# A decoder step on one core: the second column block's weights are loaded ahead of the query, key and value weights

## The chip, the core and the metric

The kernel runs on one core of a Trainium2 chip. A core has a tensor engine (PE, which multiplies and transposes; PEld is its loading of weights), a vector engine (DVE), a scalar engine (ACT), a general engine (POOL, which also starts the indirect gathers) and an engine that starts the ordinary DMA transfers (SP). Each works through its own list of instructions in order, and waits on the others by semaphores. The metric is the device time of one execution in microseconds (us).

## The reference

One layer of a decoder, for a prompt of 1024 tokens and for a sample of 8 sequences with 8 new tokens each, which also read 8192 cached positions in pages:

```
n = rmsnorm(h, g_mix)
u = n @ w_in                                     # one projection: columns of GLA q, k, v, gate, rank; MLA latents
gq, gk, gv, gg, ga, mq, mkv, mkr = split(u)
o_gla = rmsnorm(gla_chunked(gq, gk, gv, decay(ga))) * silu(gg)
qf = rmsnorm(mq) @ mla_w_qup                     # 8 heads: 64 plain + 32 rotary columns, each normalised
ckv, krope = rmsnorm(mkv), rope(rmsnorm(mkr))
k, v = from ckv @ mla_w_kvup, krope              # also for every cached page of the sample
o_mla = attention(q, k, v)
h = h + [o_gla, o_mla] @ w_o
h = h + conv_ffn(rmsnorm(h))                     # gated, causal convolution of width 3
h = h + (p @ ple_w_proj) * sigmoid(rmsnorm(h) @ ple_w_gate)
```

## The kernel before

**Arithmetic.** Products are made in fp32r, with each operand split into a high and a low part. `split` casts the high part on ACT (L138) and subtracts it from the source on DVE, or on POOL where the caller says so (L139). `mm3` then makes three matmuls: high by high (L162), low by high (L163), high by low (L164).

**Two streams.** The program is written as two generators. The cache stream goes over 64 blocks of the paged cache (8 sequences of 8 blocks). Per block it gathers 128x1024 values (`craw`) and 128x256 (`krraw`) through POOL's queue (L496), transposes them (L545), multiplies them by the key weights (`ks`, L162 to L164), and does scores (`csr`), exponentials and sums; `chl` (L626 on ACT, L628 on POOL) is the split of a block's latents for its last product, 128x1024 elements. The dense stream makes the first and the second half of the prompt (`prompt_half(0)`, `prompt_half(1)`), then GLA and prompt attention. A loop takes a step of the one or the other: each dense step yields a number (7.2, 2.0, ...) that says how much of the tensor engine it is worth, and the cache stream's due time advances by 4.4 times a pace per step. This sets the order in which the program is written. A scheduler then gives each engine its list: of the instructions that are ready by its own estimate, the one written first goes first. So a load that is written earlier has precedence over those that are now written behind it, on SP and, with its cast and its subtraction, on ACT and POOL.

**The half prompt.** `prompt_half` normalises and transposes the tokens into `xTh`, `xTl` (8 x 128 rows by 512 tokens), makes the latents `lat` (`ps_lt`), and goes on by column blocks of `w_in` of 128 columns. `load_mix` fetches a block's weights with two DMAs of 128x4x128 (256 KB each, L180, into `stage`), casts them on ACT and subtracts on POOL; the product `ps_pj` is eight steps of `mm3`, 128x512 each. In the first half, each block is also multiplied by the sample's rows (`ps_sm`, L309); `gsf` (L313, L315) gathers the result, and `pt_gvs` (L854) transposes it. The order is given by `PLAN`:

```
PLAN = ([0], [], [1, 2, 3])
```

Block 0 comes first, then `rank()` (`pt_ga`, L869), the norms of the latents, the loads of the query weights (`load_q`: four pieces of 128x384, L180, low parts on DVE) and of the key and value weights (`load_kv`: two pieces of 128x512, DVE), and then, for each tile of 128 tokens, the transposes of its latents (`latents_T`: `pt_cq`, L925), one column block (1, 2, 3, and none with the last tile) and the tile's heads (`ps_q`, `ps_kv`). The weight tiles `w` share a pool of three buffers, the `stage` tiles one of three.

**The sample's opening.** In the first half, the sample's query is made between block 0 and block 1. `q_finish` normalises it on DVE: `rsqrt` (L123, L124, L125 on `nwt`, `qrs`), then the plain part `qt` by its reciprocal norm (L350) and gain (L351), and the rotary part (L353, L354). `sample_absorb` transposes it on the tensor engine (`pt_q`, L439), copies it on ACT to `qT_s` (L440), multiplies it by the absorbed key weights (`ps_qp`, L443), and transposes the rotary part (`pt_qr`, L449). The casts of L454 on POOL (`mv1h`, `mv1l`) copy the split key weights for the odd sequences.

Of the kernel before, what the change touches and what calls it, by code (L numbers as in the profile page):

```python
# [18 lines left out]
P = 128  # L19
# [48 lines left out]
def step_kernel(ctx: ExitStack, tc: tile.TileContext, A):  # L68
# [97 lines left out]
    def wload(wp, src, kc, n, tag, bufs=None, sbufs=2, st=None, lo_eng=None, out=None):  # L166

        if out is None:
            hi = wp.tile([P, kc, n], F32R, tag=tag + "h", name=tag + "h", bufs=bufs)
            lo = wp.tile([P, kc, n], F32R, tag=tag + "l", name=tag + "l", bufs=bufs)  # L170
        else:
            hi, lo = out
        sv = src.rearrange("(k p) c -> p k c", p=P)
        nc_ = n if n <= 512 else (512 if n % 512 == 0 else 384)
        ks = max(d for d in range(1, kc + 1) if kc % d == 0 and d * nc_ <= 512)
        for k0 in range(0, kc, ks):
            for c0 in range(0, n, nc_):
                raw = st([P, ks, nc_], F32) if st else wp.tile([P, ks, nc_], F32, tag="stage", name="stage", bufs=sbufs)
                cs = slice(c0, c0 + nc_)
                sp.dma_start(raw, sv[:, k0:k0 + ks, cs])  # L180
                split(hi[:, k0:k0 + ks, cs], lo[:, k0:k0 + ks, cs], raw, lo_eng)
        return hi, lo
# [77 lines left out]
    def wtile():  # L260
        return wp.tile([P, 2 * D], F32R, tag="w", name="w")

    def wpair(kc, n):

        w = wtile()
        return tuple(w[:, s * kc * n:(s + 1) * kc * n].rearrange("p (k c) -> p k c", c=n) for s in range(2))

    def load_q():
        return [wload(wp, A["mla_w_qup"][0][:, f * 384:(f + 1) * 384], 2, 384, "w", sbufs=3, out=wpair(2, 384))
                for f in range(2)]  # L270

    def load_kv():
        hl = [wk.tile([P, 1, D], F32R, tag="xin", name="wkv") for _ in range(2)]
        return [w[:, 0] for w in wload(wp, A["mla_w_kvup"][0], 1, D, "w", sbufs=3, out=hl)]

    def load_mix(c0, lo_eng=pool):

        w = wtile().rearrange("p (k s c) -> p k s c", k=8, s=2)
        hl = wload(wp, w_in[:, c0:c0 + P], 8, P, "w", sbufs=3, lo_eng=lo_eng, out=(w[:, :, 0], w[:, :, 1]))
        return hl + (w,)  # L280
# [255 lines left out]
    turned_c, ahead, loads = [], [0], [0]  # L536
# [204 lines left out]
    def prompt_half(hf):  # L741
# [5 lines left out]
        def proj(w, n, st=None):  # L747
            ps = pd([P, 512], "ps_pj")
            for k in range(8):
                mm3(ps[:n], w[0][:, k, :], w[1][:, k, :], xTh[:, k, :], xTl[:, k, :], k == 0, k == 7)  # L750
            if st is None:
                st = wk.tile([P, 512], F32, tag="st", name="st", bufs=3)
            act.copy(st[:n], ps[:n])
            return st
# [78 lines left out]

        def gates(G, G0):

            with tc.high_priority():
                for x in [G, ggs] + G0:
                    tc.keep_in_program_order(act.activation(x, x, AF.Silu))
                tc.keep_in_program_order(act.preload_act_table_set("natural_log_exp_and_others"))
            put_gates(G, hs)  # L840
            for x, t in zip(G0, (0, 256)):
                put_gates(x, slice(t, t + 256))

        def put_gates(G, ts):
            sp.dma_start(dgg[:, ts].rearrange("(c p) t -> p c t", p=P), G)

        def post(c, st, w, G=None):
            c0 = c * P
            if c < 4:
                sp.dma_start(dgqk[c0:c0 + P, hs], st)  # L850
            if hf == 0:
                t = proj_sample(w, pd)
                pt = pd([P, 512], "pt_gvs")
                pe.transpose(pt[:, :R], t, ident[:R, :R])  # L854
                act.copy(gqT[:, c, :] if c < 4 else ggs[:, c - 8, :], pt[:, :R])
                if c == 11:
                    put_gates(G, hs)
            elif c == 8:
                for t in (0, 256):
                    x = wk.tile([P, 4, 256], F32, tag="xin", name="G0")  # L860
                    sp.dma_start(x, dgg[:, t:t + 256].rearrange("(c p) t -> p c t", p=P))
                    G0.append(x)

        G0 = []

        def rank():
            pt = pd([P, 4, P], "pt_ga")
# [7 lines left out]
        def norm_latents(i):  # L875
            t = 4 * hf + i
            tt = slice(t * P, (t + 1) * P)
            l = lat[:, i, 16:NL]
            latents(l, P, ropep[:, t, :], l[:, 0:256], l[:, 256:384], l[:, 384:416])
            sp.dma_start(A["ckv_p"][tt, :], l[:, 256:384])  # L880
            sp.dma_start(A["krope_p"][tt, :], l[:, 384:416])

        def mix(chunks, G=None):
            prev = None
            for c in chunks + [None] * bool(chunks):
                if c is not None:
                    w = load_mix(c * P)
                    st = proj(w, P, G[:, c - 8] if c >= 8 else None)
                    if c == 11 and hf > 0:
                        gates(G, G0)  # L890
                if prev is not None:
                    post(*prev, G)
                prev = (c, st, w)
                yield (5.3 if hf else 7.2) if c is not None else 0.3
# [36 lines left out]
        def heads(i, cTh, cTl):  # L931
# [31 lines left out]
            yield 1.3  # L963

        yield from mix(PLAN[0])
        rank()
        for i in range(4):
            norm_latents(i)
        yield from mix(PLAN[1])
        wq = load_q()  # L970
        wkh, wkl = load_kv()
        for i in range(4):
            cT = latents_T(i)
            yield from mix(PLAN[2][i:i + 1])
            yield from heads(i, *cT)
# [403 lines left out]
    def dense():  # L1379
        for hf in range(2):  # L1380
            z["part"] = 2 * hf
            if hf:
                z["gla"] = gla_weights()
            yield from prompt_half(hf)
        den.close()
        wa2 = const.tile([17, 256], F32, tag="gtile", name="wa2")
        sp.dma_start(wa2[0:1], A["gla_b_a"])
        sp.dma_start(wa2[1:17], A["gla_w_a2"][0])
        with ExitStack() as s2:
            g, g2 = (s2.enter_context(tc.tile_pool(name=nm, bufs=2, reuse_waits="tile")) for nm in ("g", "g2"))  # L1390
            z["part"] = 4
            sample = gla_sample(g, wa2, *z["gla"])
            for n, w in enumerate(gla_prompt(g2, wa2, *z["gla"])):
                yield w
                if n > GS0:
                    z["part"] = 5
                    w2 = next(sample, None)
                    if w2 is not None:
                        yield w2
            for w in sample:  # L1400
                yield w
        with ExitStack() as s2:
            ap = s2.enter_context(tc.tile_pool(name="ap", bufs=2, reuse_waits="tile"))
            z["part"] = 6
            yield from prompt_attention(ap)
        z["part"] = 7
        wo_room()
# [229 lines left out]
    while live_c or live_d:  # L1637
# [4 lines left out]
        else:  # L1642
            w = next(dn, done)
# [307 lines left out]
    with tc.issue_after(z["phl"].ins):  # L1951
# [4 lines left out]
        for i, r in enumerate(raws45):  # L1956
            f, c = i // 2, 4 + i % 2
# [888 lines left out]
```

## Time and profile before

| | before |
|---|---|
| runs, us | 2199.25, 2199.87, 2206.59 (median 2199.87) |
| the profiled execution, us | 2198.96 |
| its span, us | 2197.3 |
| mean granted clock of the tensor engine | 0.987 |
| PEld busy | 1901.9 us, 87% |
| DMA | 244.55 MB, 111 GB/s over the span |

The span goes from the first to the last instruction of the profiled execution; its own time is 1.7 us more. A busy time is the sum over an engine's instructions; the share is of the span. In a list of instructions in order of time, a row gives start, duration (us), engine, line, operation, result<-operands, size, type, count, and in brackets how long the engine had stood idle before and which instruction released it. In a list of waits, the three numbers behind a row are the idle time, how often, and the longest. In a table by stretches, a row gives the stretch (us), its length, then busy time and number of instructions of PE, PEld, DVE, ACT and POOL, then PE's granted clock, the share of DMA and GB/s.

### The profile page before, as it was taken

What the parts mean: (1) busy time and instruction counts of PE and PEld (TensorE: products, weight loads), DVE (VectorE), ACT (ScalarE), POOL (GpSimd) and SP (SyncE); (2) the same over time, 40 slices, a digit from 0 to 9 for tenths busy, and PEclk for the clock granted to TensorE, in tenths of its full rate; (3) what the DMA queues carried; (4) which work ended last, traced back from release to release, by engine and by line L of the source; (5) the groups of instructions that cost most, each with busy time, mean ns of one, the idle gap of its engine ahead of it and who ended that gap; (6) DMA issues with size and microseconds to landing.
All of it is one profiled execution on the core that took longest, in us unless ns stands there. A gap on an engine that the chain in (4) does not pass through costs nothing. (4 is left out here: it accounts for less than half of the span.)

```text
span 2197.3 us, 37407 instructions
## 1 busy us (share of the span) xinstructions
PE 2121.5 (97%) x12928; PEld 1901.9 (87%) x12928; DVE 1704.0 (78%) x2611; ACT 1384.2 (63%) x3735; POOL 1229.4 (56%) x1348
## 2 busy tenths in 40 slices
PE   7999999999999999999999999999999999999998
PEld 6888978878888888887898978999999999888787
DVE  4775667377778888887788888788888886887795
ACT  5676766777778888887777776443333334434761
POOL 6675668576677777767454656556566562011211
PEclk9999999999999999999999999999999999999999
DMA  5343245422342222221431223232322325778642
GB/s 184 109 142 111 72 124 159 131 70 61 104 125 65 61 68 66 62 62 42 164 91 61 68 74 118 90 110 82 98 91 93 100 92 193 221 219 245 195 145 84
DMA packets 203576, 244.55 MB, mean 111 GB/s; under 512 B 42940, under 2 KB 137260, under 8 KB 203388
## 3 DMA queue, kind: packets, MB, share of 16 engines
q1 hardware_dynamic: 184428, 181.39, 26.3%
q0 software_dynamic: 17728, 56.31, 8.7%
q10 hardware_dynamic: 1232, 4.46, 0.6%
q8 instruction: 104, 1.70, 0.3%
q14 instruction: 84, 0.69, 0.1%
HBM read 196.39 MB, written 45.67 MB: 110 GB/s over the span
## 5 line engine op out<-in xcount | busy, mean ns | idle before, releaser
L583 ACT ACTIVATE csq<-ks 128x256 f32<-128x256 f32 x1040 | 392.8, 401 | 93.7 <-PE ks L164 82.0
L588 DVE TENSOR_REDUCE css<-csq 128x16 f32<-128x1024 f32 (+1 forms) x264 | 315.7, 1196 | 60.4 <-ACT csq L583 59.2
L138 ACT CAST wh<-st 128x512 fp32r<-128x512 f32 x164 | 100.9, 619 | 169.9 <-PE ps_gu L163 157.6
L162 PE MATMUL ks<-mv0h,cTh 128*128 128x320 f32 (+1 forms) x520 | 171.5, 332 | 7.4 <-ACT sn L585 3.7
L162 PE MATMUL ks<-mv1h,cTh 128*128 128x320 f32 (+1 forms) x520 | 170.1, 329 | 7.6 <-ACT sn L585 3.6
L628 POOL TENSOR_TENSOR chl<-craw,chl 128x1024 fp32r<-128x1024 f32 x64 | 141.5, 2211 | 55.4 <-ACT chl L626 54.8
L163 PE MATMUL ks<-mv1l,cTh 128*128 128x320 f32 (+1 forms) x520 | 153.8, 298 | 0.0
L163 PE MATMUL ks<-mv0l,cTh 128*128 128x320 f32 (+1 forms) x520 | 152.7, 295 | 0.0
L164 PE MATMUL ks<-mv0h,cTl 128*128 128x320 f32 (+1 forms) x520 | 148.2, 298 | 0.9 <-DVE cTl L139 0.8
L164 PE MATMUL ks<-mv1h,cTl 128*128 128x320 f32 (+1 forms) x520 | 148.4, 299 | 0.1
L656 POOL TENSOR_TENSOR phl<-sn,phl 128x512 fp32r<-128x512 f32 (+1 forms) x63 | 84.0, 1334 | 83.1 <-ACT phl L653 82.6
L139 DVE TENSOR_TENSOR wl<-st,wh 128x512 fp32r<-128x512 f32 x124 | 108.6, 879 | 25.8 <-ACT wh L138 25.7
L139 POOL TENSOR_TENSOR wl<-st,wh 128x512 fp32r<-128x512 f32 x40 | 62.0, 1550 | 104.9 <-ACT wh L138 100.1
L163 PE MATMUL ps_dn<-o 128*128 128x512 f32 x308 | 120.2, 390 | 0.1
L164 PE MATMUL ps_dn<-o 128*128 128x512 f32 x308 | 120.2, 390 | 0.0
L139 DVE TENSOR_TENSOR cTl<-ctp,cTh 128x512 fp32r<-128x512 f32 (+1 forms) x136 | 90.0, 662 | 37.5 <-ACT cTh L138 36.5
L162 PEld LDWEIGHTS ks<-mv0h,cTh 128*128 128x128 f32 x520 | 98.6, 190 | 21.4 <-ACT sn L585 8.1
L585 ACT COPY sn<-ks 128x64 f32<-128x64 f32 x520 | 116.8, 225 | 0.0
L162 PEld LDWEIGHTS ks<-mv1h,cTh 128*128 128x128 f32 x520 | 99.3, 191 | 19.8 <-ACT sn L585 7.4
L1333 POOL TENSOR_TENSOR pl<-p,ph 128x512 fp32r<-128x512 f32 (+1 forms) x96 | 97.5, 1020 | 32.7 <-DVE ph L1332 22.7
L162 PE MATMUL ps_dn<-o 128*128 128x512 f32 x308 | 115.8, 391 | 0.0
L164 PE MATMUL ps_gu<-xrh,wl 128*128 128x320 f32 x352 | 108.8, 309 | 0.0
(744 smaller groups left out, 7760.9 us busy)
## 6 DMA issues: line engine op xcount, KB each, us to landing
raw<-ds SPq DMA_DIRECT2D x77, 256.0 KB
raw<-ffn_w_down SPq DMA_DIRECT2D x66, 256.0 KB
stage<-w_in SPq DMA_DIRECT2D x48, 256.0 KB
wr<-ffn_w_down SPq DMA_DIRECT2D x44, 256.0 KB
st<-ffn_w_gate SPq DMA_DIRECT2D x42, 256.0 KB
st<-ffn_w_up SPq DMA_DIRECT2D x42, 256.0 KB
ds<-cv SPq DMA_DIRECT2D x19, 512.0 KB
oraw<-doT SPq DMA_DIRECT2D x16, 256.0 KB
```

Source lines behind the costliest of these rows:

```text
L138: cast = act.copy(hi, src)
L139: res = (lo_eng or dve).tensor_tensor(lo, src, hi.bitcast(F32), ALU.subtract)
L162: pe.matmul(ps, ah, bh, start=first, stop=False)
L163: pe.matmul(ps, ah, bl, start=False, stop=False)
L164: return pe.matmul(ps, al, bh, start=False, stop=last)
L583: act.activation(sq[:, f * 256:f * 256 + 256], ks[:, 0:256], AF.Square)
L585: act.copy(o.sn[:, g0 + i, :], ks[:, 256:320])
L588: dve.tensor_reduce(o.ss[:, g0 + i + 1 - n:g0 + i + 1, :].rearrange("p i h -> p (i h)"), sq2[:, :n].rearrange("p i (h n) -> p (i h) n", n= ...
L628: pool.tensor_tensor(ch[:, c0:c1, 128:256], src, ch[:, c0:c1, 0:128].bitcast(F32), ALU.subtract)
L656: (dve if drain == 2 else pool).tensor_tensor(phl[:, :nt, 64:128], sb, phl[:, :nt, 0:64].bitcast(F32), ALU.subtract)
L1333: pool.tensor_tensor(pl[:, c0:], p[:, c0:], ph[:, c0:].bitcast(F32), ALU.subtract)
```

## The change

In the first half of the prompt, the weights of column block 1 are loaded ahead of the query, key and value weights, and kept until the block's turn comes; its product stays where it was written, behind the transposes of the first tile's latents. The second half is as before.

```diff
--- before.py
+++ after.py
@@ -861,7 +861,7 @@
                     sp.dma_start(x, dgg[:, t:t + 256].rearrange("(c p) t -> p c t", p=P))
                     G0.append(x)
 
-        G0 = []
+        G0, ahead = [], {}
 
         def rank():
             pt = pd([P, 4, P], "pt_ga")
@@ -884,7 +884,7 @@
             prev = None
             for c in chunks + [None] * bool(chunks):
                 if c is not None:
-                    w = load_mix(c * P)
+                    w = ahead.pop(c) if c in ahead else load_mix(c * P)
                     st = proj(w, P, G[:, c - 8] if c >= 8 else None)
                     if c == 11 and hf > 0:
                         gates(G, G0)
@@ -967,6 +967,8 @@
         for i in range(4):
             norm_latents(i)
         yield from mix(PLAN[1])
+        if hf == 0:
+            ahead[1] = load_mix(P)
         wq = load_q()
         wkh, wkl = load_kv()
         for i in range(4):
```

Every engine gets the same instructions as before, in another order: on the tensor engine from the first `pt_cq` on, up to about its 6300th of 12692 instructions, and the same from there on. Lines behind L970 are two higher in the changed kernel.

On SP the loads of the block come ahead of those of the query weights (the numbers behind `stage` count the tiles as the program writes them):

```order
-L180 DMA stage_893<-mla_w_qup 128x384
+L180 DMA stage_893<-w_in 128x4x128
 L382 DMA krope_s<-krs_117 64x32
 L503 DMA newk_111<-krs_117 8x32
 L422 DMA wkr_554<-mla_w_kvup 128x1024
-L180 DMA stage_897<-mla_w_qup 128x384
+L180 DMA stage_897<-w_in 128x4x128
 L180 DMA stage_902<-mla_w_qup 128x384
 L180 DMA stage_906<-mla_w_qup 128x384
```

The first two query pieces made room, and are now issued behind these rows.

On POOL, in the opening, the subtractions of the block (`w_892`) come between the gather of a cache block and the casts of L454, ahead of L628:

```order
 L496 DMA craw_719<-cache_ckv,idx_114 128x1024
+L139 TENSOR_TENSOR w_892<-stage_893,w_892 128x4x128
 L454 CAST mv1h_100<-mv0h_98 128x256 x2
-L454 CAST mv1l_101<-mv0l_99 128x256 x2
+L454 CAST mv1l_101<-mv0l_99 128x256
+L139 TENSOR_TENSOR w_892<-stage_897,w_892 128x4x128
+L454 CAST mv1l_101<-mv0l_99 128x256
 L131 TENSOR_SCALAR rs_v_813<-ss3_809 128x3
 L628 TENSOR_TENSOR chl_106<-craw_636,chl_106 128x8x128
```

Both stand ahead of L628 now; they stood far behind it.

On DVE, the sample's query is finished here (`nwt`, `qrs`, `qt`), between subtractions of query weights (`w_892` to `w_910`). Before:

```order
L139 TENSOR_TENSOR w_892<-stage_897,w_892 128x384
L139 TENSOR_TENSOR w_901<-stage_902,w_901 128x384
L123 TENSOR_TENSOR nwt_538<-qrs_537 64x16
L124 SCALAR_TENSOR_TENSOR nwt_538<-nwt_538,qss_524 64x16
L125 SCALAR_TENSOR_TENSOR qrs_537<-nwt_538,qrs_537 64x16
L139 TENSOR_TENSOR w_901<-stage_906,w_901 128x384
L350 TENSOR_TENSOR qt_523<-qt_523,qrs_537 64x8x64
L353 TENSOR_TENSOR qt_523<-qt_523,qrs_537 64x8x32
L351 TENSOR_TENSOR qt_523<-qt_523,gqk_73 64x8x64
L313 TENSOR_TENSOR gsf_792<-ps_sm_783,gsf_792 64x128
L354 TENSOR_TENSOR qt_523<-qt_523,gtile_72 64x8x32
```

After:

```order
L139 TENSOR_TENSOR w_901<-stage_902,w_901 128x384
L123 TENSOR_TENSOR nwt_538<-qrs_537 64x16
L124 SCALAR_TENSOR_TENSOR nwt_538<-nwt_538,qss_524 64x16
L125 SCALAR_TENSOR_TENSOR qrs_537<-nwt_538,qrs_537 64x16
L350 TENSOR_TENSOR qt_523<-qt_523,qrs_537 64x8x64
L353 TENSOR_TENSOR qt_523<-qt_523,qrs_537 64x8x32
L313 TENSOR_TENSOR gsf_792<-ps_sm_783,gsf_792 64x128
L351 TENSOR_TENSOR qt_523<-qt_523,gqk_73 64x8x64
L139 TENSOR_TENSOR w_901<-stage_906,w_901 128x384
L354 TENSOR_TENSOR qt_523<-qt_523,gtile_72 64x8x32
L315 TENSOR_TENSOR gsf_792<-ps_sm_783,gsf_792 64x128
```

One subtraction less stands ahead of L123 and one less ahead of L350; L313 has moved ahead of L351, and a subtraction stands between L351 and L354.

On PE, behind block 0's products, the transposes of the sample's query, `rank`, the latents and block 1's product (`ps_pj_937`) follow each other. Before:

```order
L439 MATMUL pt_q_600<-ident_61,qt_523 64x64 x8
L854 MATMUL pt_gvs_796<-ident_61,gsf_792 128x64
L869 MATMUL pt_ga_799<-ident_61,lat_170 16x128 x4
L925 MATMUL pt_cq_920<-ident_61,lat_170 128x128 x3
L443 MATMUL ps_qp_610<-qT_s_599,WkT_560 128x64 x8
L162 MATMUL ps_pj_937<-xTh_168,w_928 128x512
```

After:

```order
L439 MATMUL pt_q_600<-ident_61,qt_523 64x64 x8
L854 MATMUL pt_gvs_796<-ident_61,gsf_792 128x64
L869 MATMUL pt_ga_799<-ident_61,lat_170 16x128 x4
L443 MATMUL ps_qp_610<-qT_s_599,WkT_560 128x64 x8
L449 MATMUL pt_qr_622<-ident_61,q4_620 128x64 x8
L925 MATMUL pt_cq_929<-ident_61,lat_170 128x128 x2
L162 MATMUL ps_pj_937<-xTh_168,w_892 128x512
```

`ps_qp` and `pt_qr` now stand ahead of `pt_cq`, and `pt_qr` ahead of the block's product, where it stood in the middle of it.

## The prediction

> **What bounds the kernel now.** I read the page's busy times first, then who waited for whom on PE, then PE's granted clock in stretches, and last the order of time on each engine from 43 to 76 us, where the change acts.
>
> ```profile
> span 2197.3 us, 37407 instructions
> PE 2121.5 (97%) x12928; PEld 1901.9 (87%) x12928; DVE 1704.0 (78%) x2611; ACT 1384.2 (63%) x3735; POOL 1229.4 (56%) x1348
> ```
>
> PE is busy for 2121.5 of 2197.3 us, so the sum of the matmuls is the bound, and the change adds and removes none. What can move is PE's idle time (75.8 us in all) and the time it runs at a lower clock. The waits of PE in the first 300 us, longest first:
>
> ```profile
> PE pt_q L439 <- DVE qt L351: 3.6, 1, 3.6
> PE ps_pj L162 <- ACT w L138: 2.4, 1, 2.4
> PE csr L164 <- DVE kTl L139: 1.5, 1, 1.5
> PE ps_qp L443 <- ACT qT_s L440: 0.9, 1, 0.9
> ```
>
> The 3.6 us lie in the opening, and their releaser is the sample's query `qt` on DVE, not a weight. The one wait for a weight (2.4 us) is elsewhere:
>
> ```profile
> 57.55 0.95 PE L439 MATMUL pt_q<-ident,qt 64*64 64x64 f32 x8 [3.62 <-DVE qt L351]
> 61.22 3.67 PE L443 MATMUL ps_qp<-qT_s,WkT 64*128 64x64 f32 x16 [0.93 <-ACT qT_s L440]
> 64.81 0.79 PE L162 MATMUL ps_pj<-xTh,w 128*128 128x512 f32 x1
> ...
> 69.94 0.39 PE L162 MATMUL ps_pj<-xTh,w 128*128 128x512 f32 x1
> ...
> 282.42 0.30 PE L164 MATMUL csr<-qbd1h,kTl 128*128 128x64 f32 x1 [1.49 <-DVE kTl L139]
> ...
> 285.74 0.80 PE L162 MATMUL ps_pj<-xTh,w 128*128 128x512 f32 x1 [2.38 <-ACT w L138]
> ```
>
> The second column block's product starts at 64.81 without a wait, right behind `ps_qp`; its fifth of eight steps starts at 69.94. The same product of the second half of the prompt, which the change doesn't touch, waits 2.38 us at 285.74. PE's clock is in the last three numbers of each row but two (PEclk, 1.00 is full speed):
>
> ```profile
> 53.90:57.55 3.65, 0.03 (x2) 0.03 (x1) 3.58 (x9) 2.55 (x10) 3.46 (x4) 1.00 0.55 184
> 57.55:61.00 3.45, 2.74 (x16) 1.75 (x16) 3.45 (x11) 1.95 (x8) 1.28 (x1) 0.51 0.46 152
> 61.00:64.50 3.50, 3.29 (x16) 3.29 (x16) 3.32 (x14) 2.15 (x6) 3.16 (x5) 0.50 0.30 67
> 64.50:68.00 3.50, 3.50 (x10) 2.73 (x10) 3.28 (x13) 1.11 (x2) 1.78 (x6) 0.52 0.36 91
> 68.00:76.00 8.00, 8.00 (x53) 6.86 (x52) 3.11 (x7) 3.56 (x8) 6.00 (x22) 1.00 0.46 133
> 280.00:292.00 12.00, 8.12 (x33) 6.29 (x33) 6.03 (x10) 5.77 (x18) 3.33 (x4) 0.72 0.69 201
> ```
>
> The idle stretch ahead of `pt_q` is followed by half clock up to 68: 10.3 us, worth 5.15 us of work. At 280 to 292 a clock of 0.72 means 12 x 0.28 x 2 = 6.7 us at half, worth 3.4.
>
> **What the moved load was late for.** On ACT and POOL, the casts and splits of the second block's two weight pieces, and what SP and DMA did for them:
>
> ```profile
> 59.03 0.62 ACT L138 CAST w<-stage 128x512 fp32r<-128x512 f32 x1 [2.55 <-DMA stage<-w_in]
> 65.60 0.62 ACT L138 CAST w<-stage 128x512 fp32r<-128x512 f32 x1 [2.45 <-DMA stage<-w_in]
> ...
> 66.30 1.28 POOL L139 TENSOR_TENSOR w<-stage,w 128x512 fp32r<-128x512 f32 x1 [1.72 <-ACT w L138]
> ...
> 44.86 3.25 SPq L180 DMA_DIRECT2D stage<-mla_w_qup  x3
> ...
> 76.99 0.45 PE L162 MATMUL ps_q<-w,lTh 128*128 128x384 f32 x1
> ```
>
> The second piece is split at 67.58; the product needs it from 69.94. So the load had 2.4 us to spare, and bringing it forward gives PE nothing directly: that term is 0, because the product stays behind `pt_q`, `ps_qp` and now also `pt_qr`. What is left is what the moved pieces push aside.
>
> **DVE and POOL, the step that I expect to decide.** The chain that releases `pt_q` is L123, L124, L125, L350, L353, L351 on DVE:
>
> ```profile
> 52.36 0.56 DVE L139 TENSOR_TENSOR w<-stage,w 128x384 fp32r<-128x384 f32 x1 [2.55 <-ACT w L138]
> 52.83 2.16 DVE L123 TENSOR_TENSOR nwt<-qrs 64x16 f32<-64x16 f32 x1
> ...
> 55.79 0.68 DVE L350 TENSOR_TENSOR qt<-qt,qrs 64x512 f32<-64x512 f32 x1
> 56.39 0.41 DVE L353 TENSOR_TENSOR qt<-qt,qrs 64x256 f32<-64x256 f32 x1
> 56.73 0.68 DVE L351 TENSOR_TENSOR qt<-qt,gqk 64x512 f32<-64x512 f32 x1
> 57.33 0.28 DVE L313 TENSOR_TENSOR gsf<-ps_sm,gsf 64x128 f32<-64x128 f32 x1
> 57.53 0.41 DVE L354 TENSOR_TENSOR qt<-qt,gtile 64x256 f32<-64x256 f32 x1
> ...
> 83.62 0.18 DVE L123 TENSOR_TENSOR nwt<-qrs 128x16 f32<-128x16 f32 x1 [0.71 <-ACT qrs L122]
> ...
> 48.84 1.79 POOL L496 DMA_INDIRECT craw<-cache_ckv,idx  x1 [0.30 <-issue]
> 50.64 0.75 POOL L454 CAST mv1h<-mv0h 128x256 fp32r<-128x256 f32 x2
> 52.15 0.25 POOL L131 TENSOR_SCALAR rs_v<-ss 128x3 f32<-128x3 f32 x1
> 52.48 2.49 POOL L628 TENSOR_TENSOR chl<-craw,chl 128x1024 fp32r<-128x1024 f32 x1
> ...
> 53.79 0.51 ACT L138 CAST w<-stage 128x384 fp32r<-128x384 f32 x1 [0.87 <-DMA stage<-mla_w_qup]
> ```
>
> L123 takes 0.18 us at 83.62, on twice the rows, and 2.16 at 52.83: it ends at 54.99, POOL's L628 at 54.97. A POOL instruction that reads two tiles holds such a DVE instruction up until it is done, and POOL gets in between two DVE instructions. Now the two moved splits stand on POOL ahead of L628. POOL is free at 50.63; a split takes 1.28, two casts 0.75, one more 0.37: the second split runs from 53.03 to 54.3. With the last cast (0.37) and L131 (0.25) L628 wants to start at 55.0.
>
> On DVE one cast piece of the query weights is left ahead of L123, at about 52.5 as before. Then L123 is held by the second split until 54.3, L123 to L125 take some 0.4 and L350 0.68, to 55.4. There L628 gets in and holds L353 up until 57.6 (2.2 us, what L628 held L123 for, 2.16). L353, L313 (moved ahead of L351) and L351 take 0.41, 0.28 and 0.68: 59.0, against 57.41 before. So `pt_q` starts some **1.5 us later**. Least: only L351 is behind L628, started at 55.0, so 57.2 + 0.7: +0.5. Most: the first query piece (issued where the third was, near 47.3) lands as late as the fourth did, 53.79: another +0.5, so +2.0.
>
> Behind `pt_q`, `pt_gvs` needs L315, which now stands behind a split (0.56), L354 (0.41) and takes 0.28 itself, while `pt_q` covers 0.74: half a microsecond of idle. The wait of `ps_qp` for `qT_s` (0.93) goes, since `pt_ga` now covers that copy: **-0.4**.
>
> On SP the two loads of the block take the places of the first two query loads (the second at 44.86), and the query and key/value loads move back past them and one store. They land some 5 us later, and `ps_q`, their first reader, runs at 76.99. ACT's casts of them stand ahead of the copy of `qT_s`; the third should land by 57, before `pt_q`. Cost 0; with that cover gone it is what ACT waited for one piece, 2.5 us. POOL's own queue of gathers stays ahead of both splits: 0.
>
> The dense product then starts near 66.5 instead of 64.81. Before, the clock came back 3.2 us behind that start. If it follows the start, half clock lasts 1.7 us longer: **+0.9**. Bounds: 0 (it doesn't follow), and 1.8 (a whole step, half of 10.3 - 6.7).
>
> The Trainium skill (TensorE: Matmul & The Clock Gate, Part 1) lets the clock return after one busy window of about 3.4 us. The trace disagrees: PE was busy 3.29 of 3.50 us from 61.0 to 64.5 and stayed at 0.50 to 68. By the page this term would be 0 and the sum 0.9 lower; the row decides.
>
> **The rest.** From 76 us on the cache stream and the dense steps share PE:
>
> ```profile
> 76.00:100.00 24.00, 24.00 (x153) 21.98 (x152) 16.12 (x34) 17.88 (x62) 14.07 (x17) 1.00 0.40 132
> ...
> 360.00:1020.00 660.00, 643.78 (x4515) 562.16 (x4514) 507.05 (x836) 537.18 (x1636) 477.35 (x539) 1.00 0.28 81
> ```
>
> PE has no idle to lose at first. The order differs from here to the end of the dense stages, about the middle of the program, by tens of matmuls, and is then the same again. In the second half the cache stream is some ten products ahead. What this does to single waits I can't read; I take 0. Bounds: the stall at 280 to 290 goes, 1.49 + 2.38 + 3.4 = -7.2; or another dense stretch stands as bare as the opening's, 3.62 + 0.93 + 5.15 = +9.7.
>
> **Sum.** 1.5 - 0.4 + 0.9 + 0 = +2.0. The profiled execution took 2198.96 us, 1.7 us beside its span and 0.9 under the median of the runs: 2198.96 + 2.0 + 0.9 = **2202**.
>
> **Rivals.**
> - POOL comes too late or DVE too early for the two to meet. Then `pt_q` starts near 55.5 (52.5 + 0.56 + 0.4 + 0.68 + 0.41 + 0.28 + 0.68), idle is 1.6 us and half clock doesn't set in: -2.05 - 0.4 - 5.15 = -7.6, so 2192. For it: the piece of DVE ahead of L350 is gone. Against: POOL's rows follow each other from 48.84 on, and its two splits and L628 are 4.8 us beside a chain of 2.5.
> - The stall of the second half goes, because more cache products stand ahead of its second block: 2202 - 7.2 = 2195. For it: ten products more; against: their evictions stand on ACT behind the casts that wait for the same loads.
> - Both together: 2185.
> - Slower: the cache products that now run early are missing later as cover, and one dense stretch lies bare. It decides where PE is left without a ready matmul for over 3 us, as at 53.9, so that half clock sets in; that is +9.7, so 2212, and two such are 2221. For it: at 280 to 286 waits of 1.49 and 2.38 were enough. Against: from 360 to 1020 PE idles 16 of 660 us.
> - The change does nothing that PE feels: `pt_q` at the old time, 2200; inside the first case, as is half clock that ends no later than before, 2201 (the rule of the page above would have it so): 0.15 of its chance.
>
> **Chances.** First case 0.46 (2198 to 2208), DVE free 0.12, second-half stall gone 0.10, both 0.12, slower 0.20. Within 0.5% (11 us, about what a measurement of this kernel can tell from no change) lie the first three: 0.68. Faster 0.12, slower 0.20. Leaving out half of each outer case and what lies beyond, the range is 2188 to 2216.
>
> **What would show it.** Right: in the profile after, L628 starts behind 54.5, one of L353 or L351 takes over 1.5 us, PE idles 4 to 5.5 us ahead of `pt_q`, the casts of the second block stand near 46 and 48 us, and half clock lasts to 68 or beyond. Wrong: `pt_q` before 57, a full clock at 60, or a change of over 5 us in PE's idle time between 100 and 1070.

## The result, and the profile after

The changed kernel takes 2210.97 us (median of 13 runs, 2206.80 to 2216.83), against 2197.59 us for the kernel before (13 runs, 2194.85 to 2209.58). The ratio is 1.0057, with an interval of 1.0045 to 1.0070: **12.5 us slower**, or 0.57%, about the 0.5% that the prediction took as the limit of what can be told; a change of zero lies outside the interval. The time lies in the predicted range (2188 to 2216), but only because the range takes in half of the rival "slower" (2212): the case held likeliest (2198 to 2208, with 2202 as the forecast) did not come about.

The head of the page of the kernel after, whose profiled execution took 2210.97 us:

```profile
span 2209.0 us, 37466 instructions
PE 2121.6 (96%) x12928; PEld 1900.0 (86%) x12928; DVE 1701.9 (77%) x2611; ACT 1384.8 (63%) x3735; POOL 1228.5 (56%) x1348
```

PE is busy 2121.6 us (before 2121.5), at a mean granted clock of 0.988 (before 0.987). Its idle time went from 75.8 to 87.4 us: that is, but for 0.1 us, the 11.7 us by which the span grew.

**Where it is lost.** In the order of time on PE, an instruction that stands at the same place of both kernels' work, the first `ps_dn`, of before and then of after:

```profile
1064.12 0.40 PE L1449 MATMUL ps_dn<-wdh,sh 128*128 128x512 f32 x1
```
```profile
1077.68 0.40 PE L1451 MATMUL ps_dn<-wdh,sh 128*128 128x512 f32 x1
```

The kernel after is 13.6 us late there and 11.7 at the end. So the loss is complete by 1064 us, where the prompt's attention ends; what comes behind it (a wait of 3.98 us at 1085 among it) adds nothing on balance. In the two profiles PE's rows are the same again from the 6770th of 12928 on, at 1073 us of the kernel before. The table by stretches says how it builds up (behind the stretch and its length stands PE's busy time; four stretches of before, then of after):

```profile
100.00:240.00 140.00, 136.25 (x930) 125.07 (x929) 94.95 (x154) 99.20 (x311) 88.10 (x86) 1.00 0.35 114
240.00:300.00 60.00, 55.30 (x314) 49.57 (x312) 37.99 (x75) 37.99 (x122) 36.49 (x44) 0.94 0.33 97
300.00:400.00 100.00, 94.04 (x575) 84.27 (x576) 71.32 (x122) 68.32 (x211) 79.28 (x88) 0.97 0.45 138
860.00:1060.00 200.00, 193.01 (x1300) 168.10 (x1299) 160.24 (x257) 166.97 (x492) 146.94 (x154) 0.98 0.20 57
```
```profile
100.00:240.00 140.00, 133.25 (x895) 122.10 (x894) 86.30 (x149) 96.20 (x301) 89.56 (x93) 0.99 0.35 109
240.00:300.00 60.00, 58.89 (x370) 54.04 (x369) 46.79 (x89) 45.71 (x148) 40.08 (x50) 1.00 0.37 105
300.00:400.00 100.00, 88.32 (x540) 79.13 (x539) 72.19 (x118) 66.15 (x206) 74.94 (x78) 0.97 0.42 132
860.00:1060.00 200.00, 190.43 (x1253) 162.40 (x1253) 157.87 (x257) 163.03 (x474) 144.86 (x148) 0.98 0.19 55
```

Idle time of PE (length less busy): 3.0 us more from 100 to 240, 3.6 less from 240 to 300, 5.7 more from 300 to 400, 2.6 more from 860 to 1060. The stall of the second half that the prediction quoted (280 to 290) has gone, and the stretch's clock has risen with it from 0.94 to 1.00; more than that is lost before and behind it. PE's longest waits from 100 to 400 us, after:

```profile
PE csr L162 <- DVE cTl L139: 4.6, 2, 2.9
PE ps_kv L162 <- ACT qt L343: 4.6, 2, 2.8
PE ks L162 <- ACT csq L583: 3.7, 5, 1.3
PE ks L162 <- ACT sn L585: 3.0, 3, 1.6
```

Before, the third and the fourth stood at 1.2 and 1.4 us, the second at 0.6, and the first wasn't among the ten longest; its own longest were 2.6 (`mt` on DVE) and the 2.4 of the stall. What came instead are a dozen waits of up to three microseconds, on DVE and on ACT, of cache products (`csr`, `ks`) and a dense one (`ps_kv`). No single wait is the loss; from 100 to 1064 us the longest is 2.92.

**The opening.** PE, DVE, POOL and ACT of the kernel after, in order of time on each engine:

```profile
58.40 1.03 PE L439 MATMUL pt_q<-ident,qt 64*64 64x64 f32 x8 [4.94 <-DVE qt L351]
65.36 0.78 PE L162 MATMUL ps_pj<-xTh,w 128*128 128x512 f32 x1
77.34 0.44 PE L162 MATMUL ps_q<-w,lTh 128*128 128x384 f32 x1
...
51.97 1.77 DVE L139 TENSOR_TENSOR w<-stage,w 128x384 fp32r<-128x384 f32 x1 [2.97 <-ACT w L138]
54.45 2.67 DVE L350 TENSOR_TENSOR qt<-qt,qrs 64x512 f32<-64x512 f32 x1
...
52.05 1.27 POOL L139 TENSOR_TENSOR w<-stage,w 128x512 fp32r<-128x512 f32 x1
54.41 2.17 POOL L628 TENSOR_TENSOR chl<-craw,chl 128x1024 fp32r<-128x1024 f32 x1
...
48.04 0.62 ACT L138 CAST w<-stage 128x512 fp32r<-128x512 f32 x1
```

The casts of the second block's two pieces now stand at 45.95 and 48.04 (59.03 and 65.60 before), and its product starts at 65.36 (64.81 before) without a wait: the earlier load gives PE nothing. POOL's split of it (52.05, 1.27 us) runs beside DVE's split of a query piece (1.77 us, where 0.56 was its time before), and POOL's L628, which held L123 before, now holds L350 (2.67 us, 0.68 before). The transpose `pt_q` starts at 58.40, 0.85 us later. At the first `ps_q` the kernel after is 0.35 us late. By this pair of profiles the opening is nearly even; the loss comes behind it.

### The profile page after: what moved, and what is told of

The parts are those of the page before. It is cut to its first block, busy times and chain, and to the rows that moved or that the text cites. A ratio compares the mean times of both kernels' runs of the same rounds, so it can differ in the third digit from the quotient of the medians.

```text
span 2209.0 us, 37466 instructions
## 1 busy us (share of the span) xinstructions
PE 2121.6 (96%) x12928; PEld 1900.0 (86%) x12928; DVE 1701.9 (77%) x2611; ACT 1384.8 (63%) x3735; POOL 1228.5 (56%) x1348
## 5 line engine op out<-in xcount | busy, mean ns | idle before, releaser
L162 PE MATMUL ks<-mv0h,cTh 128*128 128x320 f32 (+1 forms) x520 | 170.7, 330 | 12.5 <-ACT sn L585 8.2
L628 POOL TENSOR_TENSOR chl<-craw,chl 128x1024 fp32r<-128x1024 f32 x64 | 141.5, 2212 | 53.0 <-ACT chl L626 52.3
L615 POOL TENSOR_TENSOR sn<-sn,cy 128x512 f32<-128x512 f32 (+1 forms) x64 | 70.7, 1105 | 74.4 <-DVE cy L613 62.1
```

The source lines that it names most:

```text
L162: pe.matmul(ps, ah, bh, start=first, stop=False)
L615: pool.tensor_tensor(snv, snv, y[:, :nt].rearrange("p i h -> p (i h)").unsqueeze(2).broadcast_to([P, nt * 8, 8]), ALU.mult)
L628: pool.tensor_tensor(ch[:, c0:c1, 128:256], src, ch[:, c0:c1, 0:128].bitcast(F32), ALU.subtract)
```

## The experiments

The change does two things: it loads and splits a block early, and, since the scheduler's list is made anew, it puts the instructions of every engine in another order up to the middle of the program. To part the two, the order was fixed: each kernel got a list of instruction numbers, and ahead of the passage in which the order was written by hand already

```diff
+    for n in ORDER:                              # numbers in the wanted order
+        i = by[n]
+        tc.add_manual_dep(i, last[i.engine], NoSync)   # order on its engine, no wait
+        last[i.engine] = i.name
```

so that each engine issues exactly in the list's order, and waits for data as before. A list can follow the one kernel up to some instruction and then the other (what is already issued is left out). The edits below name only the list. Differences are against the kernel before, run on the same chip beside them.

**Opening alone: the change up to 79 us, then the old order.**

```diff
-ORDER = after's
+ORDER = after's up to the first tile's last ps_q (79 us), then before's
```

> The change's code, with the order of each engine's instructions fixed: up to the first tile's query product (79 us) as in the changed kernel, behind that as before. Theory A (the order behind the opening costs the time): the opening alone was 0.4 us late at that product, so 0 to +2 us against before. Theory B (the moved load and its splits cost it in the opening, by what they push aside): +10 to +13 us, as the whole change.

Measured: 0.9993 (0.9982 to 1.0004), -1.5 us (-4.0 to +0.9). The moved load, with all that it does on DVE, POOL, SP and ACT in the opening, costs nothing that can be measured; +2.0 is left out by the interval. Nor does a fixed list by itself add time that shows.

**The new order behind the opening, with no load moved.**

```diff
-ORDER = before's
+ORDER = before's up to 79 us, then after's
```

> The code before, with the order of each engine fixed: up to the first tile's query product (79 us) as before, behind that as in the changed kernel. Nothing is loaded ahead. Theory A: slower by +10 to +13 us although the change isn't in it. Theory B: 0 to +2 us.

Measured: 1.0048 (1.0034 to 1.0061), +10.5 us (7.5 to 13.4). The code is that of the kernel before, the second block's load stands where it stood, and most or all of the loss is there. In its profile PE waits 0.5 us in all from 70 to 130 us, so hardly anything is lost where the one list goes over into the other. This settles the first question: the slowdown is the order of the rest.

**Where in the rest.** Further switches, new order first:

```diff
+ORDER = after's up to 118 us, then before's            # new_to_118
+ORDER = after's up to 238 us (first half), then before's    # new_to_238
+ORDER = after's up to the end of the second half, then before's   # new_to_438
```

> The change's code; order as in the changed kernel up to the third tile's query product (118 us), behind that as before. Between 98 and 118 us the changed order puts cache work ahead of the second tile's query on POOL (its gain L351 starts at 109.1 instead of 103.9 us), and cache products ahead of the third tile's on PE. Theory E (this choice spends the cover that is missing at 126 to 150 us): +3 to +4 us against before, most of the first half's loss. If the loss is made by the order behind 118 us: 0 to +1.

> The change's code; order as in the changed kernel up to the end of the first half of the prompt (238 us), behind that as before. Theory A1 (the waits of the first half, first that of ps_kv at 138 us, make the loss): work stood 5 to 6 us late there, so +4 to +7. Theory A2 (it is made in the second half, at 320 to 400 us): 0 to +2, or a gain, should the rest not suffer. Theory B: +10 to +13.

> The change's code; order as in the changed kernel up to the end of the second half of the prompt (some 450 us), behind that as before. By the work done at equal times the changed kernel stood 7 to 8 us late there. Theory A1 or A2: +6 to +9, so that a third of the loss is made behind it, in GLA and prompt attention. Theory A3 (most of it is made there): under +4.

Measured: +1.3 us (-0.7 to 3.3), +5.0 (3.1 to 7.3) and +9.7 (6.6 to 12.5). The loss grows with the length of the new order: between 118 and 238 us by some 4. The last number can't be read as a loss of the second half: in its trace PE waits 8.26 us at the switch itself (at 449.73, `ps_z` for the load of `gaT`), where it waits 2.4 us in the kernel before and 2.6 in the kernel after.

Old order first:

```diff
+ORDER = before's up to 238 us, then after's                       # old_to_238
+ORDER = before's up to 640 us (end of GLA), then after's           # old_to_640
```

> The code before, nothing loaded ahead; order as before up to the end of the first half of the prompt (238 us), behind that as in the changed kernel. Places that add up: the whole +10.6 less the +5.0 of the first half, +4 to +7 us. If the later waits only follow from the first half's delay: 0 to +2. If what is won early is lost again behind it: +9 or more.

> The code before, nothing loaded ahead; order as before up to the last transpose of GLA's output (640 us), behind that, through prompt attention to 1070 us, as in the changed kernel. In the run that took the changed order from 238 us on, PE lost some 8 us of work-equal time in the second half of the prompt and GLA, and 6 to 8 us more between 760 and 1040 us. If the order in prompt attention costs by itself: +4 to +8 us. If it costs only because the dense stages came late there: -1 to +2.

Measured: +13.4 us (10.3 to 16.5) and +8.3 (5.1 to 11.7). The parts don't add: 5.0 up to 238 and 13.4 behind it would be 18.4, where the whole loses 12.5. The first of these runs also loses at its switch:

```profile
241.02 2.09 PE L671 MATMUL cpv<-chl,phl 128*128 128x258 f32 x8 [2.34 <-POOL phl L656]
248.75 1.23 PE L155 MATMUL pt<-ident,xw 128*128 128x128 f32 x8 [1.94 <-DVE xTl L139]
```

With one of 0.95 at 229 us these are 5.2 us of waits from 222 to 262, where the kernel before waits 0.82 and the kernel after 1.00. The excess, some 4 us, can account for most of what the sum has too much; so +13.4 is likely more than the new order behind 238 us costs in its own place. In the prompt's attention, the kernel before, then the old order up to 640:

```profile
880.00:940.00 60.00, 58.39 (x401) 50.96 (x402) 50.82 (x86) 52.36 (x154) 42.62 (x48) 1.00 0.21 57
```
```profile
880.00:940.00 60.00, 55.49 (x372) 47.02 (x372) 51.26 (x78) 48.06 (x143) 43.67 (x47) 1.00 0.21 58
```

PE idles 4.5 of 60 us instead of 1.6, at full clock. Its waits from 860 to 1040 are of at most 1.4 us each, on DVE and ACT for the most part. So the new order loses in the first half and in the attention separately.

**The stretch that the change won.** The second half's stall was rid of by the new order; does it pay alone?

```diff
+ORDER = before's, but from 238 to 307 us in after's order
```

> The code before, nothing loaded ahead; order as before, but from 238 to 307 us as in the changed kernel, where the stall of 280 to 290 us is missing. By the work done at equal times the changed kernel won 8 us there. Theory A (only the order counts, place by place): 5 to 8 us faster than before, 2190 to 2193. If the stall's end depends on what went ahead, or is paid back behind it: 2196 or more.

Measured: 1.0016 (1.0003 to 1.0030), +3.5 us (0.7 to 6.6). It didn't pay. Three stretches, of the kernel before and of this one:

```profile
220.00:260.00 40.00, 39.10 (x276) 37.60 (x276) 25.63 (x40) 31.06 (x100) 25.15 (x32) 1.00 0.29 86
260.00:300.00 40.00, 36.12 (x199) 31.30 (x197) 26.23 (x57) 24.71 (x76) 20.14 (x21) 0.91 0.34 100
300.00:340.00 40.00, 37.73 (x225) 33.22 (x226) 34.81 (x64) 29.03 (x95) 32.49 (x46) 1.00 0.38 123
```
```profile
220.00:260.00 40.00, 35.96 (x260) 34.06 (x259) 26.57 (x41) 30.58 (x91) 22.18 (x29) 1.00 0.31 86
260.00:300.00 40.00, 39.95 (x245) 36.58 (x244) 31.06 (x66) 29.75 (x102) 27.73 (x37) 1.00 0.33 94
300.00:340.00 40.00, 35.51 (x183) 30.10 (x182) 25.01 (x49) 23.54 (x75) 25.32 (x32) 0.96 0.37 119
```

In the middle 3.8 us of idle go, and the clock rises from 0.91 to 1.00 (40 x 0.09 = 3.6 us more). The stretch ahead idles 3.1 us more, the one behind 2.2, at a clock of 0.96 (1.6). Added up, hardly anything is left of the gain. At a `ps_gv` product behind the stretch (361.15 before, 362.51 here) this execution is 1.4 us late, and it was 0.5 late ahead of it, at 223 us; it was the fastest of its 12 runs (2195.72), so its profile can't show the whole of the 3.5. The 3.1 us ahead are three waits (0.95, 1.69 and 1.25 us, from 228 to 245) where the list goes over to the new order, and most of the idle behind is one wait of 2.90 (`ps_kv` at 319.89) soon after it goes back; in these places the two kernels wait 0.82 and 1.00 us, and 1.45 and nothing. So the run shows that the stretch pays nothing when it is put in like this. Whether its cover was taken from its neighbours, or the gain went at the two switches, it doesn't tell.

**A control.**

```diff
-PACE = [1.41, 1.088, 1.601, 1.168, 1.142, 0.708, 1.035, 1.027]
+PACE = [1.42, 1.088, 1.601, 1.168, 1.142, 0.708, 1.035, 1.027]
```

> The code before with one number of the pacing changed from 1.41 to 1.42; no load is moved, and the scheduler makes its order anew. Theory A (an order that comes out otherwise moves the time by several us, whatever made it): 2 to 12 us away from before, more likely slower. If an order is worth little by itself and only the moved load made this one bad: within 2 us.

Measured: 1.0000 (0.9991 to 1.0008). This run says less than it was meant to. The program is written a little differently, but the rows of PE, DVE, ACT and POOL come out the same, one for one; so it tests no new order. What it shows is the measurement: the same lists give the same time within 2 us either way, while the profile of a single execution (2195.83 us, against 2198.96) differs by 3. Whether another order would as a rule lose is therefore open. The opening of this execution, from PE's first `ps_q` and a stretch ahead of it:

```profile
77.46 0.44 PE L162 MATMUL ps_q<-w,lTh 128*128 128x384 f32 x1
68.00:72.00 4.00, 4.00 (x24) 2.89 (x23) 1.42 (x3) 1.17 (x2) 2.54 (x10) 0.88 0.33 82
```

With the lists of the kernel before, `ps_q` comes 0.47 us later than in the kernel before (76.99), and half clock goes on beyond 68 us.

**Taking the largest waits away.** In the kernel after, PE waits 2.81 us for `qt` at 141 us and 2.92 for `cTl` at 328. At the first, PE, ACT, SP and POOL:

```profile
141.08 0.62 PE L162 MATMUL ps_kv<-wkv,lTh 128*128 128x512 f32 x1 [2.81 <-ACT qt L343]
140.55 0.86 ACT L343 COPY qt<-ps_q 128x384 f32<-128x384 f32 x2 [1.86 <-DMA dk<-kt]
137.87 0.34 SPq L961 DMA_DIRECT2D dk<-kt  x1
143.06 0.38 SPq L942 DMA_DIRECT2D dq<-qt  x1
137.25 1.72 POOL L351 TENSOR_TENSOR qt<-qt,gqk 128x512 f32<-128x512 f32 x1
```

POOL makes three weight splits before it comes to the third tile's query gain (L351 at 137.25, 129.16 before). The query's store goes out late (143.06, 135.87 before) and now behind the key's (137.87, 138.64 before), and ACT's copy into the same buffers waits for the key's.

```diff
+ORDER = after's, but POOL's L351, L354 of this tile ahead of the weight split,
+        DVE's L198 to L201 ahead of a reduction, SP's dq store ahead of dk
```

> The changed kernel with its own order fixed, but for the third tile's query in the first half: its gain (L351, L354) goes ahead of a weight split on POOL, its rotation (L198 to L201) ahead of a reduction on DVE, and its store ahead of that of the key on SP, as they stood before. Theory C (at 138 us ps_kv waits 2.81 us because the tile's query leaves late and the next takes the key's buffer; half clock follows): that wait falls under 1 us and 3 to 4 us are won, 2206 to 2208. If the loss only moves to the next wait: 2210 or more.

Measured: 1.0061 (1.0046 to 1.0077), +13.4 us (10.1 to 16.9), as the kernel after. The wait of 2.81 shrank to 0.84, and another came 3 us ahead of it:

```profile
137.75 0.58 PE L162 MATMUL ks<-mv0h,cTh 128*128 128x256 f32 x1 [3.40 <-ACT sn L585]
136.70 0.62 ACT L138 CAST w<-stage 128x512 fp32r<-128x512 f32 x1 [3.22 <-DMA stage<-w_in]
```

With POOL's splits later, the `stage` buffers come free later, the next load starts later, ACT's cast of it waits 3.22 us, and the copies of the cache's `ks` behind it on ACT hold PE. At the second place, PE and DVE:

```profile
328.37 0.35 PE L162 MATMUL csr<-qbd1h,kTh 128*128 128x256 f32 x1 [2.92 <-DVE cTl L139]
326.18 1.44 DVE L201 TENSOR_TENSOR qt<-rqa,rqb 128x256 f32<-128x256 f32 x1
327.54 0.68 DVE L139 TENSOR_TENSOR cTl<-ctp,cTh 128x512 fp32r<-128x512 f32 x1
```

At 141 us of the same kernel L199 takes 0.28 us and L201 0.42; here they take 1.37 and 1.44, with two splits and L628 of POOL beside them, from 322.37 to 327.34. The split `cTl` stands behind them.

```diff
+ORDER = after's, but DVE's split cTl (L139) ahead of L198
```

> The changed kernel with its own order fixed, but for one instruction: on DVE the low part of the cache latents (L139 cTl) that PE waits 2.92 us for at 328 us goes ahead of the query's rotation, whose four short instructions took 1.4 us each beside POOL's splits there. Theory C: the wait goes, with half clock behind it; 3 to 5 us are won, 2206 to 2208. If the loss only moves: 2210 or more.

Measured: 1.0065 (1.0052 to 1.0079), +14.3 us (11.4 to 17.4). Again the wait only moved, to the next instruction of the same chain on DVE:

```profile
330.10 0.38 PE L164 MATMUL csr<-qbd1h,kTl 128*128 128x256 f32 x1 [3.53 <-DVE kTl L139]
```

Of both expectations the gain failed: where the one wait was taken away, another of 3.4 or 3.5 us stood close by. That the chain behind them is late as a whole is how this reads. A third buffer for `qt`, which would uncouple ACT's copy from the stores, was not tried.

**DVE freed in the opening.** If the order is held, is the moved load worth something once POOL keeps off DVE's chain?

```diff
-ORDER = after's up to 79 us, then before's
+ORDER = the same, but POOL's second split of the block (L139) behind the first
+        small pair of L134, and L628 behind the next L134
```

> As the run with the changed order up to 79 us, but on POOL the block's second split (L139) and the cache block's split L628 are moved behind two pairs of the latents' norms (L131, L134), out of the query's way. Theory P (a large two-operand instruction of POOL holds up DVE: L350 took 2.67 us and a weight split 1.77 beside them): both take their usual 0.7 and 0.6 us, pt_q starts near 55.6 instead of 58.4 us, and PE idles some 2 us there instead of 4.9; the time falls by 2 to 3 us, by 5 more if half clock does not set in. If DVE was slow for another reason: L350 stays above 2 us and the time is the same.

Measured: 0.9983 (0.9974 to 0.9992), 2193.94 us against 2197.48: **-3.7 us** (-5.7 to -1.8). This version is faster than the kernel before. PE, DVE and POOL:

```profile
55.28 0.60 PE L439 MATMUL pt_q<-ident,qt 64*64 64x64 f32 x8 [1.75 <-DVE qt L351]
57.82 0.36 PE L854 MATMUL pt_gvs<-ident,gsf 64*128 64x64 f32 x1 [1.93 <-DVE gsf L315]
52.04 0.56 DVE L139 TENSOR_TENSOR w<-stage,w 128x384 fp32r<-128x384 f32 x1 [2.97 <-ACT w L138]
54.47 0.67 DVE L351 TENSOR_TENSOR qt<-qt,gqk 64x512 f32<-64x512 f32 x1
56.08 1.48 DVE L354 TENSOR_TENSOR qt<-qt,gtile 64x256 f32<-64x256 f32 x1
53.59 2.27 POOL L134 TENSOR_TENSOR rs_r<-rs_v,mhalf 128x3 f32<-128x3 f32 x2
55.83 1.46 POOL L139 TENSOR_TENSOR w<-stage,w 128x512 fp32r<-128x512 f32 x1
```

DVE's split takes 0.56 again and its query chain runs through (L350, the long one of the kernel after, in 0.68), while POOL is busy with the small L134 (128x3), beside which L351 takes its 0.67. `pt_q` starts at 55.28, 3.1 us earlier than in the kernel after. A part is lost again: POOL's split now meets L354 (1.48 us, 0.41 before), `gsf` behind it comes late, and `pt_gvs` waits 1.93 us; and PE's clock still falls to 0.50 (from 58 to 61 us, and 0.74 from 64.5 to 68). The first `ps_q` is at 75.03, 2.0 us ahead of the kernel before. Against the opening alone (-1.5) the gain is 2.2, with intervals that overlap; against the kernel before it is outside its uncertainty. So the gain is that of the moved load and the freed DVE together. How it divides between them is open: no run frees DVE with the load left where it was.

## Why the prediction was right and wrong

**Right: the direct gain of 0.** The block's product starts at 65.36 against 64.81, with no wait ahead of it in either kernel.

**Right in kind: DVE and POOL.** POOL's split and then L628 hold instructions of DVE's query chain. The prediction had L628 start at 55.0 and hold L353 or L351; it started at 54.41 and held L350, so two of the signs named for it (a start behind 54.5, L353 or L351 over 1.5 us) are missing. PE's idle ahead of `pt_q` was 4.94 us (4 to 5.5 were named), and `pt_q` came 0.85 us later than before (1.5; 0.5 to 2.0). This execution was 0.46 us ahead of the other from before the change acts (a split on POOL at 43.07 instead of 43.53, `ps_sm` at 52.84 instead of 53.30); counted from there, the idle grew by 1.3 us. Which instruction L628 holds also varies without a change: with the same lists, it held L123 in the kernel before (2.16 us), and in the control the split ahead of it (2.29 us). The wait of `ps_qp` for `qT_s` (-0.4) did go. The half microsecond ahead of `pt_gvs` isn't in the kernel after.

**Half clock (+0.9).** Stretches of the kernel after:

```profile
61.00:64.50 3.50, 3.50 (x21) 3.50 (x21) 3.22 (x13) 2.52 (x10) 1.52 (x2) 0.50 0.65 178
64.50:68.00 3.50, 3.50 (x14) 2.76 (x13) 2.40 (x10) 0.96 (x2) 3.06 (x9) 0.50 0.41 102
68.00:72.00 4.00, 4.00 (x19) 3.29 (x18) 2.74 (x14) 0.85 (x2) 3.36 (x14) 0.80 0.40 107
...
328.40:332.00 3.60, 3.60 (x16) 3.38 (x17) 2.69 (x6) 1.57 (x6) 2.61 (x5) 0.59 0.91 291
```

At 0.80 over 4 us, half clock lasts 1.6 us beyond 68: to 69.6, worth 0.8. That the term has its size is luck. In the control, whose lists are those of the kernel before, the clock is 0.88 over the same 4 us: half clock lasts 1.0 us beyond 68 with no change at all. The opening's whole is +0.35 at `ps_q`, or +0.8 counted from `ps_sm`; the control took 1.3 us longer than the kernel before for the same stretch (from 52.50 to 77.46). So one pair of profiles can't tell these terms, and the run that has the opening alone gives -1.5, not +2.0.

By the Trainium skill (TensorE: Matmul & The Clock Gate, Part 1) full clock returns after at least one busy window of about 3.4 us, and what is issued behind that time runs at full clock. The opening contradicts it again: PE is busy without a gap from 58.4 to 69.6, 11.2 us, and stays at 0.50. Behind the wait at 328 us it agrees: half clock there takes 3.6 x 0.41 x 2 = 3.0 us of the stretch.

**The step that failed: "the rest, I take 0".** It measured +10.5 us by itself, above its upper bound of +9.7, though the interval (7.5 to 13.4) still holds the bound. The prediction saw that the order differs to the middle of the program and priced it by the two events it could read, one stall that goes and one stretch that lies bare. The stall went as the rival had it, and more than that was lost ahead of it and behind it. The rival "slower" named a cause that fits the waits (cache products spent early are missing as cover later) and almost the time (2212), but not the shape: from 100 to 400 us there is not one bare stretch of over three microseconds with half clock behind it, but a dozen shorter waits. So its time came true by another sum than its own (3.62 + 0.93 + 5.15), and that is luck. That PE had no idle at first, and idled 16 of 660 us later, was taken as a reason against the rival; it says only that little can be won there, and nothing of what can be lost. The sign named to show the prediction wrong, over 5 us in PE's idle time between 100 and 1070, is there, with 37.9 us before and 43.6 after:

```profile
100.00:1070.00 970.00, 932.06 (x6316) 819.95 (x6314) 721.27 (x1201) 749.92 (x2289) 681.07 (x763) 0.99 0.31 90
```
```profile
100.00:1070.00 970.00, 926.38 (x6251) 812.90 (x6249) 708.83 (x1187) 741.13 (x2255) 678.20 (x759) 0.99 0.30 88
```

**The rival "DVE free" (2192)** is not what the change did, but the run that made it so took 2193.9. Its `pt_q` starts at 55.28 and waits 1.75 us (55.5 and 1.6 were named); half clock, which by the rival doesn't set in, still did.

**Open.** Shown is that the order behind the opening carries the loss, that it loses in the first half and in the attention separately, and that taking either of its two longest waits away doesn't win it back. Why this order is worse isn't brought to one cause, and how much of the +13.4 from 238 us on is the switch of lists isn't measured. That cache products come early and are missing later is how the waits read; no run took that by itself.

## What to carry to other kernels

Where a scheduler lists the instructions, moving one load changes the list of every engine far behind it: measure the moved load with the rest of the order held, and the new order with the load left where it was. Look for waits where one list goes over into the other, since they belong to neither kernel. A new order that can't be read from the trace is not a zero; here it cost some 10 us of 2200, and whether new orders lean to slower can't be told from one. Two large two-operand POOL instructions kept off the DVE chain that PE waits for, with the load moved, were worth 3.7 us here; the moved load without that was worth nothing that could be measured.

## What the runs showed of the hardware

A POOL instruction that takes long doesn't always hold DVE: L628 (128x1024, 2.17 us) stretched L350 from 0.68 to 2.67, and a split of 128x512 (1.27 us) a DVE split from 0.56 to 1.77, while beside the pair of L134 (128x3, 2.27 us from 53.59) L351 took its usual 0.67. With the two large ones moved away, both DVE instructions took their usual time. The Trainium skill (SBUF — State Buffer, "SBUF: two separate sides") has the first two as an exclusive lock on ports that the two engines share, held for the whole instruction. The trace agrees there: L628 ends at 56.58, and L350, which started with it, 0.54 later. By the page the one that starts first has the ports; DVE's split started at 51.97, 0.08 ahead of POOL's, and was stretched all the same. The page doesn't tell the small instruction apart.
